# Attention scores from stacked key halves in two fp32r passes, in a two-layer decoder trunk

## The chip, the cores and the metric

The kernel runs on one core of a Trainium2 chip. Its engines run their own instruction streams side by side: TensorE (PE, matmuls; PEld are its weight loads), VectorE (DVE), ScalarE (ACT), GpSimd (POOL) and SyncE (SP), which issues most DMAs. GpSimd and ScalarE issue some too, each on a queue of its own. The metric is the device time of one execution in microseconds (us).

## The reference

Two layers over 512 tokens of width 1024. Each normalizes `x`, projects it to 3088 columns, splits them among three mixers (differential attention, a short gated convolution, gated linear attention), projects the three outputs back and adds them; then a PEER layer with 16384 single-neuron experts follows. What the change touches is the differential attention: four heads, each with two queries and two keys of 64 (index `m`), blocks of 128 queries, causal.

```python
for i in range(DEPTH):
    h = rmsnorm(x, norm_mix[i])
    proj = h @ w_in[i]
    ...
    # per block of 128 queries, 4 heads h, 2 halves m of 64:
    s = einsum('bqhmd,bkhmd->bhmqk', qi, k) * 64 ** -0.5
    p = softmax(where(mask, s, -inf), axis=-1)
    a = p[:, :, 0] - lam * p[:, :, 1]
    o_da = rmsnorm(einsum('bhqk,bkhe->bqhe', a, v), gain) * out_scale
    ...
    x = x + concatenate([o_da, o_sc, o_g]) @ w_out[i]
    x = x + peer(rmsnorm(x, norm_ffn[i]), peer_w_q[i], ...)
return rmsnorm(x, norm_final)
```

## The kernel before

Nearly all products are made from rounded and low halves: `split` (L83) rounds an F32 tile to fp32r on ACT (the high half) and subtracts it from the tile on DVE (the low half), and `mm3` (L77) contracts high x high, high x low and low x high, three fp32r matmuls for one F32 product (L79 to L81). The scores are an exception: they are one plain F32 call, which PE runs as two matmul instructions.

The mixer of a layer streams `w_in` in slabs of 256 columns. `slab` loads four pieces of a slab on SP's queue and splits them; `across` contracts a slab, 48 matmuls of 512 columns into two `psp` tiles; `down` does the same with tokens on the partitions. First come the slabs of the gated linear attention, whose own steps (`gla`, its matmuls at L610 to L680) are woven in by `fill`; then those of the queries and keys, written to `qT` and `kT` (partitions: the 64 entries of half 0 and then those of half 1; free: head, token), with a rotation of their first entries by copies on GpSimd's queue (`rope_pack`, `rope`, L459 to L471); then the values `va`; and then three slabs of the convolution, 2048, 1792 and 1536. Between these three stands the attention of blocks 0 and 1, with the scores of two heads of block 2. After them comes the output projection: `woraw` (two buffers) takes 128 rows of `w_out` at a time, split into `woh` and `wol`; blocks 2 and 3 of the attention run meanwhile, `head_out` turns the heads (`htr`) and splits them into `mh` and `ml`, and `out_proj` adds the products (`pso`) to `x`. The norm and the query projection of the PEER layer (`uraw` split into `uwa` or `uwb`, matmuls into `psq`) follow at once.

For a block and a head, `head_weights` (L479) makes the scores of both halves. The two halves lie on different partitions of `qT` and `kT`; to contract 128 partitions, `turned_queries` (L473) copies the 64 rows of a half into `qz`, whose other 64 rows are zero (filled once a layer, L369), so the keys of the other half meet zeros. A bfloat16 matmul of the identity with `causal` adds the mask (L487). DVE takes the maximum of each row, ACT the exponential.

The program is written in the order above, but each engine's order is made when the program is built: a scheduler merges the streams by what they depend on. SBUF is handed out by pools: a pool that closes gives its addresses to pools that open later, and the first writer of such an address waits for the last user of what lay there. `qT`, `kT` and `va` are in the pool `mix` (L226), which lasts for the whole mixer; the pools of the slabs close before `wout` (L404) opens.

Of the kernel before, what the change touches and what calls it, by code (L numbers as in the profile page):

```python
# [7 lines left out]
F32 = mybir.dt.float32  # L8
F32R = mybir.dt.float32r
# [10 lines left out]
P = 128  # L20
T = 512
# [46 lines left out]
class K:  # L68
# [152 lines left out]
    def mixer(self, L):  # L221
        nc, tc, ins = self.nc, self.tc, self.ins
        lam_init = 0.8 - 0.6 * math.exp(-0.3 * L)
        right = ExitStack()
        with ExitStack() as mc:
            mp = mc.enter_context(tc.tile_pool(name="mix", bufs=1, reuse_waits="tile"))  # L226
            dgain = mp.tile([P, 1], F32, name="dgain")
            cw = mp.tile([P, 2, 3], F32, name="cw")
            qT = mp.tile([P, 4, T], F32, name="qT")
            kT = mp.tile([P, 4, T], F32, name="kT")  # L230
            va = mp.tile([P, TB, T], F32, name="va")
            if L == 0:
                hh, hl = self.new_act()
                rows = lambda t: [t[:, 2 * i:2 * i + 2].rearrange("p a b -> p (a b)") for i in range(2)]
                norm = self.norm_T(ins["norm_mix"][L:L + 1, :], hh, hl, rows(va) + rows(kT), order=ORDER)
            else:
                hh, hl = self.hh, self.hl
            with ExitStack() as wc:
                wp = wc.enter_context(tc.tile_pool(name="wpool", bufs=2, reuse_waits="tile"))
                qp = wc.enter_context(tc.tile_pool(name="qkn", bufs=2, reuse_waits="tile"))  # L240
                mo = right.enter_context(tc.tile_pool(name="mixo", bufs=1, side="right", reuse_waits="tile"))
# [26 lines left out]
                def across(c0, n=256):  # L268
                    wh, wl = slab(c0, n)
                    for j in range(n // P):  # L270
                        ps = self.psC.tile([P, T], F32, tag="c", name="psp")
                        for k in range(KD):
                            self.mm3(ps, wh[:, k, j * P:j * P + P], wl[:, k, j * P:j * P + P], hh[:, k], hl[:, k],
                                     k == 0, k == KD - 1)
                        yield j, ps
# [15 lines left out]
                for i, tb in enumerate(ORDER):  # L291
                    if L:
                        ps = self.psv.pop(tb)
                    else:
                        next(norm, None)
                        ps = self.psC.tile([P, 256], F32, tag="c", name="psv")
# [18 lines left out]
                lam = mp.tile([P, 1], F32, name="lam")  # L315
# [4 lines left out]
                for tb in range(TB):  # L320
                    ps = self.psC.tile([P, 272], F32, tag="c", name="psp")
# [10 lines left out]
                side = self.gla(L, gq, gk, gv, sg, lr, mgh, mgl, gp)  # L332
# [13 lines left out]
                for i in range(4):  # L346
                    dst, h = (qT, kT)[i // 2], i % 2
# [16 lines left out]
                gc.close()  # L364
                ac = mc.enter_context(ExitStack())
                ap = ac.enter_context(tc.tile_pool(name="attn", bufs=2, side="right", reuse_waits="tile"))
                qz = [ap.tile([P, 4, 2, P], F32, name=f"qz{i}", bufs=1) for i in range(2)]
                for t in qz:
                    nc.gpsimd.memset(t, 0.0)  # L369
                heads = []  # L370

                def attend(tb, early=()):
                    heads.append(self.diff_attention(tb, qT, kT, va, qz[tb % 2], lam, ap, early))

                attend(0)
                z = qp.tile([P, 2, T + 2], F32, tag="z", name="z", bufs=1)
                nc.vector.memset(z[:, :, 0:2], 0.0)
                for j, ps in across(2048):
                    nc.scalar.copy(z[:, j, 2:], ps)
                attend(1)  # L380
                for j, ps in across(1792):
                    nc.vector.tensor_tensor(z[:, j, 2:], ps, z[:, j, 2:], op=OP.mult)
                nc.sync.dma_start(cw, ins["conv_w"][L])
                ys = []
                yt = qp.tile([P, 2, T], F32, tag="y", name="y", bufs=1)
# [6 lines left out]
                    ys.append(y)  # L392
                for j, ps in across(1536):
                    if j == 0:
                        self.turned_queries(2, qT, qz[0])
                        early = [self.head_weights(2, h, kT, qz[0], lam, ap) for h in range(2)]
                    nc.vector.tensor_tensor(ys[j], ys[j], ps, op=OP.mult)
                    self.split(mch[:, j], mcl[:, j], ys[j])

            with tc.tile_pool(name="wout", bufs=1, reuse_waits="tile") as op_:  # L400
# [31 lines left out]
                for tb in range(TB):  # L432
                    if tb > 1:
                        attend(tb, early if tb == 2 else ())
                    t = slice(tb * P, tb * P + P)
                    self.head_out(heads[tb], dgain, mh[:, 0:4, t], ml[:, 0:4, t])
# [33 lines left out]
            for m in range(2):  # L470
                nc.gpsimd.dma_start(dst[64 * m:64 * m + 16, 2 * h:2 * h + 2], rot[32 * h + 16 * m:32 * h + 16 * m + 16])  # L471

    def turned_queries(self, tb, qT, qz):  # L473
        s = slice(tb * P, tb * P + P)
        for m in range(2):
            r = slice(64 * m, 64 * m + 64)
            self.nc.scalar.copy(qz[r, :, m], qT[r, :, s])

    def head_weights(self, tb, h, kT, qz, lam, ap):  # L479
        nc = self.nc  # L480
        nk = (tb + 1) * P
        st = self.sm.tile([P, 8], F32, tag="st", name="st")
        pss = []
        for m in range(2):
            ps = self.psA.tile([P, T], F32, tag="a", name="pss")
            nc.tensor.matmul(ps[:, 0:nk], qz[:, h, m], kT[:, h, 0:nk], start=True, stop=False)  # L486
            nc.tensor.matmul(ps[:, tb * P:nk], self.identb, self.causal, start=False, stop=True)  # L487
            nc.vector.tensor_reduce(st[:, m:m + 1], ps[:, 0:nk], axis=AX.X, op=OP.max)
            pss.append(ps)
        nc.vector.tensor_scalar(st[:, 2:4], st[:, 0:2], -0.125, None, op0=OP.mult)  # L490
        e = ap.tile([P, 2, T], F32, tag="e", name="e")
        for m in range(2):
            nc.scalar.activation(e[:, m, 0:nk], pss[m][:, 0:nk], AF.Exp, bias=st[:, 2 + m:3 + m],
                                 scale=0.125, accum_out=st[:, 4 + m:5 + m])
        nc.vector.reciprocal(st[:, 6:8], st[:, 4:6])
        nc.vector.tensor_tensor(st[:, 7:8], st[:, 7:8], lam, op=OP.mult)
        nc.vector.tensor_scalar(e[:, 1, 0:nk], e[:, 1, 0:nk], st[:, 7:8], None, op0=OP.mult)
        nc.vector.scalar_tensor_tensor(e[:, 0, 0:nk], e[:, 0, 0:nk], st[:, 6:7], e[:, 1, 0:nk],
                                       op0=OP.mult, op1=OP.subtract)
        return e  # L500

    def diff_attention(self, tb, qT, kT, va, qz, lam, ap, early=()):
        nc = self.nc
        early = list(early)
        if not early:
            self.turned_queries(tb, qT, qz)
        po = self.psB.tile([P, 4, P], F32, tag="b", name="po")
        for h in range(4):
            e = early.pop(0) if early else self.head_weights(tb, h, kT, qz, lam, ap)
            tr = self.psB.tile([P, 4, P], F32, tag="b", name="atr")  # L510
            for kb in range(tb + 1):
                nc.tensor.transpose(tr[:, kb], e[:, 0, kb * P:kb * P + P], self.ident)
            aT = ap.tile([P, 4, P], F32, tag="aT", name="aT")
            nc.scalar.copy(aT[:, 0:tb + 1], tr[:, 0:tb + 1])
            for kb in range(tb + 1):
                nc.tensor.matmul(po[:, h], aT[:, kb], va[:, kb, h * P:h * P + P],
                                 start=(kb == 0), stop=(kb == tb))
        return self.head_norm(po, 4, P, ap)
# [763 lines left out]
```

## Time and profile before

| | |
|---|---|
| median of 3 runs | 2962.35 us (2961.81 to 2962.88) |
| profiled execution | 2958.37 us |
| its span, first to last instruction | 2956.6 us, clock 0.999 |
| busy: PE, DVE, ACT, POOL | 2925.6, 2394.7, 1256.3, 716.0 us |
| scores (first start in layer 0, last in layer 1) | 150.8 to 1682.2 us |

A row of a timeline has start, length (from the start of the first to the end of the last of its instructions), engine, line, operation, names written and read, shape and count; in brackets stand idle time before it and what ended that. Starts and lengths are us. A matmul's length includes the time that its result is still under way, so the pace of the engine is read from start to start. Windows give busy time of each engine in a stretch. In the groups of the page, idle time on an engine that is not the bottleneck costs nothing.

### The profile page before, as it was taken

What the parts mean: (1) busy time and instruction counts of PE and PEld (TensorE: products, weight loads), DVE (VectorE), ACT (ScalarE), POOL (GpSimd) and SP (SyncE); (2) the same over time, 40 slices, a digit from 0 to 9 for tenths busy, and PEclk for the clock granted to TensorE, in tenths of its full rate; (3) what the DMA queues carried; (4) which work ended last, traced back from release to release, by engine and by line L of the source; (5) the groups of instructions that cost most, each with busy time, mean ns of one, the idle gap of its engine ahead of it and who ended that gap; (6) DMA issues with size and microseconds to landing.
All of it is one profiled execution on the core that took longest, in us unless ns stands there. A gap on an engine that the chain in (4) does not pass through costs nothing.

```text
span 2956.6 us, 44538 instructions
## 1 busy us (share of the span) xinstructions
PE 2925.6 (99%) x16262; PEld 2606.0 (88%) x16262; DVE 2394.7 (81%) x4754; ACT 1256.3 (42%) x1860; POOL 716.0 (24%) x617
## 2 busy tenths in 40 slices
PE   8999999999999999999999999999999999999998
PEld 7878899999999999888888788999999999988887
DVE  6676999976887788877866769999768787888778
ACT  6253355665333332333453433556653333333333
POOL 1200000222444455222012000012225444452220
PEclk9999999999999999999999999999999999999999
DMA  4322257999999998999633222679999999989995
GB/s 130 92 72 77 93 172 250 321 301 362 348 338 326 330 346 310 368 333 342 251 96 90 67 82 86 205 253 330 303 351 356 333 337 332 332 316 358 346 347 203
DMA packets 335835, 760.24 MB, mean 257 GB/s; under 512 B 30688, under 2 KB 191360, under 8 KB 331520
## 3 DMA queue, kind: packets, MB, share of 16 engines
q1 hardware_dynamic: 160624, 435.19, 41.4%
q0 software_dynamic: 75776, 271.62, 26.0%
q10 hardware_dynamic: 99216, 50.60, 5.7%
q8 instruction: 127, 2.08, 0.3%
q14 instruction: 92, 0.75, 0.1%
HBM read 673.15 MB, written 81.00 MB: 255 GB/s over the span
## 4 chain that ended last, share of the span: by engine, by line
PE 84%; DVE 11%; ACT 2%; issue 2%; DMA 1%; SPq 0%; DVEq 0%; ACTq 0%
PE pv L80 11%; PE pv L81 11%; PE pv L79 11%; PE psh L79 9%; PE psh L81 9%; PE psh L80 9%; PE psp L80 2%; PE psp L81 2%; PE psp L79 2%; PE psq L80 2%; PE psq L79 2%; PE psq L81 2%; PE pss L486 1%; PE psg L1211 1%; PE pss L764 1%
## 5 line engine op out<-in xcount | busy, mean ns | idle before, releaser
L827 POOL DMA_INDIRECT row<-in_u_rows,idx x256 | 349.1, 1363 | 1337.6 <-DVE row L834 627.8
L80 PE MATMUL pv<-vl,wh 128*128 128x512 f32 x1500 | 583.9, 389 | 0.4 <-DVE vl L931 0.3
L81 PE MATMUL pv<-vh,wl 128*128 128x512 f32 x1500 | 583.4, 389 | 0.0
L79 PE MATMUL pv<-vh,wh 128*128 128x512 f32 x1500 | 583.2, 389 | 0.0
L827 POOL DMA_INDIRECT row<-in_v_rows,idx x256 | 315.7, 1233 | 597.0 <-DVE yacc L843 548.2
L745 ACT ACTIVATE ht<-psh 128x384 f32<-128x384 f32 x256 | 125.7, 491 | 742.1 <-PE psh L81 741.9
L931 DVE TENSOR_TENSOR vl<-vraw,vh 128x1024 fp32r<-128x1024 f32 x250 | 305.9, 1224 | 115.2 <-ACT vh L936 104.2
L79 PE MATMUL psh<-ahi,uwb 128*128 128x384 f32 x1024 | 346.9, 339 | 0.0
L79 PE MATMUL psh<-ahi,uwa 128*128 128x384 f32 x1024 | 346.4, 338 | 0.0
L81 PE MATMUL psh<-ahi,uwa 128*128 128x384 f32 x1024 | 344.6, 337 | 0.7 <-DVE uwa L730 0.7
L80 PE MATMUL psh<-alo,uwa 128*128 128x384 f32 x1024 | 344.3, 336 | 0.0
L80 PE MATMUL psh<-alo,uwb 128*128 128x384 f32 x1024 | 344.2, 336 | 0.0
L81 PE MATMUL psh<-ahi,uwb 128*128 128x384 f32 x1024 | 344.1, 336 | 0.0
L81 PEld LDWEIGHTS pv<-vh,wl 128*128 128x128 f32 x1500 | 281.4, 188 | 59.6 <-DVE wl L931 1.0
L80 PEld LDWEIGHTS pv<-vl,wh 128*128 128x128 f32 x1500 | 281.4, 188 | 56.6 <-DVE vl L931 2.2
L79 PEld LDWEIGHTS pv<-vh,wh 128*128 128x128 f32 x1500 | 281.6, 188 | 53.9
L843 DVE SCALAR_TENSOR_TENSOR yacc<-row,wk,yacc 128x1024 f32<-128x1024 f32 x254 | 325.2, 1280 | 1.7
L944 ACT CAST wh<-ht 128x384 fp32r<-128x384 f32 x250 | 127.9, 512 | 433.6 <-DVE ht L1096 417.0
L834 DVE SCALAR_TENSOR_TENSOR row<-row,xg 128x1024 f32<-128x1024 f32 x256 | 308.0, 1219 | 0.0
L730 DVE TENSOR_TENSOR uwa<-uraw,uwa 128x1024 fp32r<-128x1024 f32 x144 | 175.7, 1223 | 134.7 <-ACT uwa L729 134.5
L936 ACT CAST vh<-vraw 128x1024 fp32r<-128x1024 f32 x250 | 262.6, 1050 | 9.7 <-DMA vraw<-in_v_rows 9.7
L730 DVE TENSOR_TENSOR uwb<-uraw,uwb 128x1024 fp32r<-128x1024 f32 x144 | 175.8, 1222 | 105.9 <-ACT uwb L729 105.9
(361 smaller groups left out, 5708.6 us busy)
## 6 DMA issues: line engine op xcount, KB each, us to landing
uraw<-in_peer_u SPq DMA_DIRECT2D x256, 512.0 KB, 5.6
vraw<-in_v_rows SPq DMA_DIRECT2D x256, 512.0 KB, 6.5
G<-stg ACTq DMA_DIRECT2D x48, 1024.0 KB, 7.6
g<-G SPq DMA_DIRECT2D x32, 1536.0 KB, 10.0
H<-ht SPq DMA_DIRECT2D x144, 192.0 KB, 4.7
ht<-H SPq DMA_DIRECT2D x144, 192.0 KB, 6.5
wraw<-in_w_in SPq DMA_DIRECT2D x84, 256.0 KB, 3.2
uraw<-in_peer_w_q SPq DMA_DIRECT2D x32, 512.0 KB, 3.5
```

The source lines that it names most:

```text
L79: mm(ps, ah, bh, start=first, stop=False)
L80: mm(ps, ah, bl, start=False, stop=False)
L81: mm(ps, al, bh, start=False, stop=last)
L486: nc.tensor.matmul(ps[:, 0:nk], qz[:, h, m], kT[:, h, 0:nk], start=True, stop=False)
L730: self.last = pin(nc.vector.tensor_tensor(lo, src, hi.bitcast(F32), op=OP.subtract))
L745: pin(nc.scalar.activation(hs[c], ps, AF.Gelu))
L827: nc.gpsimd.indirect_dma_start(out=r, out_offset=None, in_=ins[name], in_offset=bass.IndirectOffsetOnAxis(ap=idx[:, k:k + 1], axis=0))
L834: nc.vector.scalar_tensor_tensor(r, r, 1.0, xg, op0=OP.mult, op1=OP.mult, accum_out=hd[:, k:k + 1])
L843: nc.vector.scalar_tensor_tensor(yacc, r, wk[:, k:k + 1], yacc, op0=OP.mult, op1=OP.add)
L931: self.last = pin(nc.vector.tensor_tensor(lo, src, hi.bitcast(F32), op=OP.subtract))
L936: pin(nc.scalar.copy(vh[c], vs[c]))
L944: pin(nc.scalar.copy(wh[c], hs[c]))
```

## The change

The zero-padded `qz` and its fills go. In their place, keys and queries are split, and the halves are stacked:

- `stack_keys(tb)` splits the keys of a block. For each half `m`, tile `ks[m]` has the rounded keys on the half's own 64 partitions; the low keys, subtracted into `klo`, are moved to the other 64 partitions by a DMA that GpSimd issues.
- `stack_queries(tb)` rounds the queries into `qa` on the half's own partitions, copies them by such a DMA to the other 64, and leaves the low queries in `qb`.
- The scores of a half are then two fp32r matmuls: `qa` with `ks[m]` over 128 partitions, which is rounded queries x (rounded + low keys), and `qb` with `ks[m]` over the 64 partitions of that half alone, which is low queries x rounded keys. Low x low is left out, as in `mm3`. The mask's matmul stays.

`qT` and `kT` move from `mix` to a pool `rawqk` that closes with the slabs. The attention of block 0 is written after slab 2048, that of block 1 after slab 1792.

```diff
-            qT = mp.tile([P, 4, T], F32, name="qT")
-            kT = mp.tile([P, 4, T], F32, name="kT")
             va = mp.tile([P, TB, T], F32, name="va")
+            wc = mc.enter_context(ExitStack())
+            raw_qk = wc.enter_context(tc.tile_pool(name="rawqk", bufs=1, reuse_waits="tile"))
+            qT = raw_qk.tile([P, 4, T], F32, name="qT")
+            kT = raw_qk.tile([P, 4, T], F32, name="kT")
...
-            with ExitStack() as wc:
+            with wc:
...
-                qz = [ap.tile([P, 4, 2, P], F32, name=f"qz{i}", bufs=1) for i in range(2)]
-                for t in qz:
-                    nc.gpsimd.memset(t, 0.0)
+                ks = [ap.tile([P, 4, T], F32R, name=f"ks{i}", bufs=1) for i in range(2)]
+                kl = wc.enter_context(tc.tile_pool(name="klow", bufs=2, side="right", reuse_waits="tile"))
+                half = [slice(64 * m, 64 * m + 64) for m in range(2)]
+
+                def stack_keys(tb):
+                    t = slice(tb * P, tb * P + P)
+                    lo = kl.tile([P, 4, P], F32R, tag="klo", name="klo")
+                    for m in range(2):
+                        r = half[m]
+                        self.split(ks[m][r, :, t], lo[r], kT[r, :, t])
+                        nc.gpsimd.dma_start(ks[m][half[1 - m], :, t], lo[r])
+
+                def stack_queries(tb):
+                    qa = ap.tile([P, 2, 4, P], F32R, tag="qa", name="qa")
+                    qb = ap.tile([P, 4, P], F32R, tag="qb", name="qb")
+                    for m in range(2):
+                        r = half[m]
+                        self.split(qa[r, m], qb[r], qT[r, :, tb * P:tb * P + P])
+                        nc.gpsimd.dma_start(qa[half[1 - m], m], qa[r, m])
+                    return qa, qb
+
                 heads = []
+                qs = {}
...
-                attend(0)
+                stack_keys(0)
+                qs[0] = stack_queries(0)
+                stack_keys(1)
+                qs[1] = stack_queries(1)
                 z = qp.tile([P, 2, T + 2], F32, tag="z", name="z", bufs=1)
                 nc.vector.memset(z[:, :, 0:2], 0.0)
                 for j, ps in across(2048):
                     nc.scalar.copy(z[:, j, 2:], ps)
-                attend(1)
+                attend(0)
+                for tb in (2, 3):
+                    stack_keys(tb)
+                qs[2] = stack_queries(2)
                 for j, ps in across(1792):
                     nc.vector.tensor_tensor(z[:, j, 2:], ps, z[:, j, 2:], op=OP.mult)
+                attend(1)
+                qs[3] = stack_queries(3)
...
                 for j, ps in across(1536):
                     if j == 0:
-                        self.turned_queries(2, qT, qz[0])
-                        early = [self.head_weights(2, h, kT, qz[0], lam, ap) for h in range(2)]
+                        early = [self.head_weights(2, h, ks, qs[2], lam, ap) for h in range(2)]
...
-    def head_weights(self, tb, h, kT, qz, lam, ap):
+    def head_weights(self, tb, h, ks, qs, lam, ap):
...
-            nc.tensor.matmul(ps[:, 0:nk], qz[:, h, m], kT[:, h, 0:nk], start=True, stop=False)
+            r = slice(64 * m, 64 * m + 64)
+            nc.tensor.matmul(ps[:, 0:nk], qs[0][:, m, h], ks[m][:, h, 0:nk], start=True, stop=False)
+            nc.tensor.matmul(ps[:, 0:nk], qs[1][r, h], ks[m][r, h, 0:nk], start=False, stop=False)
             nc.tensor.matmul(ps[:, tb * P:nk], self.identb, self.causal, start=False, stop=True)
```

PE, the first scores of layer 0 (`pss`; `psp` is slab 2048), before:

```order
674 L79 MATMUL psp<-ahi,wh 128x512
675 L486 MATMUL pss<-kT,qz_1503 128x128
676 L487 LDWEIGHTS identb
677 L487 MATMUL pss<-causal,identb 128x128
678 L80 MATMUL psp<-alo,wh 128x512
679 L486 MATMUL pss<-kT,qz_1503 128x128
680 L487 LDWEIGHTS identb
681 L487 MATMUL pss<-causal,identb 128x128
```

and the first scores in the change:

```order
705 L80 MATMUL psp<-alo,wh 128x512
706 L81 MATMUL psp<-ahi,wl 128x512
707 L509 MATMUL pss<-ks_1506,qa 128x128
708 L510 MATMUL pss<-ks_1506,qb 128x128
709 L511 LDWEIGHTS identb
710 L511 MATMUL pss<-causal,identb 128x128
711 L509 MATMUL pss<-ks_1507,qa 128x128
712 L510 MATMUL pss<-ks_1507,qb 128x128
713 L511 LDWEIGHTS identb
714 L511 MATMUL pss<-causal,identb 128x128
```

Before, the first scores stood between matmuls of slab 2048; now all 48 of that slab are ahead of them, and a pair has a second pass before its mask.

POOL, the end of layer 0's mixer (`kT<-rot` is the end of the keys' rotation, `row` the gathers of the PEER layer); in the change:

```order
49 L499 DMA kT<-rot 16x2x512 x4
50 L387 DMA qa<-qa 64x512
51 L379 DMA ks_1506<-klo 64x4x128
52 L379 DMA ks_1507<-klo 64x4x128
53 L387 DMA qa<-qa 64x512
54 L379 DMA ks_1506<-klo 64x4x128
55 L379 DMA ks_1507<-klo 64x4x128
56 L387 DMA qa<-qa 64x512 x2
```

Where these and eight more copies stand, two fills of `qz` stood before.

ACT, from the norm ahead of the PEER layer to its first weights (`ahi` is the rounded normalized `x`), with the semaphores of what each instruction waits for, before:

```order
184 L211 CAST ahi<-psn 128x4x128 [waits PE_49] x2
185 L729 CAST uwa<-uraw 128x1024 [waits DMAHW5_49]
186 L729 CAST uwa<-uraw 128x1024 [waits DMAHW6_49]
187 L729 CAST uwb<-uraw 128x1024 [waits DMAHW7_49,PE_49]
188 L729 CAST uwb<-uraw 128x1024 [waits DMAHW0_49,PE_49]
```

and in the change:

```order
194 L211 CAST ahi<-psn 128x4x128 [waits PE_49] x2
195 L751 CAST uwa<-uraw 128x1024 [waits DMAHW5_49,PE_49]
196 L751 CAST uwa<-uraw 128x1024 [waits DMAHW6_49,PE_49]
197 L751 CAST uwb<-uraw 128x1024 [waits DMAHW7_49]
198 L751 CAST uwb<-uraw 128x1024 [waits DMAHW0_49]
```

The order of the casts is the same; the first two wait for PE now, where the third and fourth did.

More of the change, by code (lines that the diff above doesn't have):

```diff
@@ L366, in mixer @@
                 ap = ac.enter_context(tc.tile_pool(name="attn", bufs=2, side="right", reuse_waits="tile"))
-                qz = [ap.tile([P, 4, 2, P], F32, name=f"qz{i}", bufs=1) for i in range(2)]
-                for t in qz:
-                    nc.gpsimd.memset(t, 0.0)
+                ks = [ap.tile([P, 4, T], F32R, name=f"ks{i}", bufs=1) for i in range(2)]
[16 more added lines that the diff above has]
+                    return qa, qb
                 heads = []
+                qs = {}
                 def attend(tb, early=()):
-                    heads.append(self.diff_attention(tb, qT, kT, va, qz[tb % 2], lam, ap, early))
-                attend(0)
+                    heads.append(self.diff_attention(tb, qs.pop(tb), ks, va, lam, ap, early))
+                stack_keys(0)
+                qs[0] = stack_queries(0)
+                stack_keys(1)
+                qs[1] = stack_queries(1)
                 z = qp.tile([P, 2, T + 2], F32, tag="z", name="z", bufs=1)
@@ L471, in rope @@
                 nc.gpsimd.dma_start(dst[64 * m:64 * m + 16, 2 * h:2 * h + 2], rot[32 * h + 16 * m:32 * h + 16 * m + 16])
[L473 to L477, printed above, removed]
-    def head_weights(self, tb, h, kT, qz, lam, ap):
+    def head_weights(self, tb, h, ks, qs, lam, ap):
         nc = self.nc
@@ L500, in head_weights, with diff_attention @@
         return e
-    def diff_attention(self, tb, qT, kT, va, qz, lam, ap, early=()):
+    def diff_attention(self, tb, qs, ks, va, lam, ap, early=()):
         nc = self.nc
         early = list(early)
-        if not early:
-            self.turned_queries(tb, qT, qz)
         po = self.psB.tile([P, 4, P], F32, tag="b", name="po")
         for h in range(4):
-            e = early.pop(0) if early else self.head_weights(tb, h, kT, qz, lam, ap)
+            e = early.pop(0) if early else self.head_weights(tb, h, ks, qs, lam, ap)
             tr = self.psB.tile([P, 4, P], F32, tag="b", name="atr")
```

## The prediction

> **What bounds the kernel now.** I read the page first, then the chain that ended last, then busy time by stage, then what TensorE (PE) waits for.
>
> ```profile
> PE   2925.6 (99%) x16262; PEld 2606.0 (88%) x16262; DVE 2394.7 (81%) x4754; ACT 1256.3 (42%) x1860; POOL 716.0 (24%) x617
> PE 84%; DVE 11%; ACT 2%; issue 2%; DMA 1%; SPq 0%; DVEq 0%; ACTq 0%
> 170.00:180.00 10.00, 10.00 (x55) 7.64 (x55) 7.84 (x23) 5.17 (x15) 0.00 (x0) 1.00 0.01 2
> 200.00:210.00 10.00, 9.38 (x48) 5.88 (x47) 9.24 (x21) 7.07 (x17) 0.00 (x0) 1.00 0.31 100
> PE pso L79 <- ACT woh L84: 0.9, 2, 0.6
> ```
>
> PE is busy for 99% of the span and carries 84% of the chain. The windows (PE, weight loads, DVE, ACT, POOL, granted clock, DMA share) say the same of the stage that the change touches: around the scores of layer 0 PE works 9.4 to 10.0 of every 10 us at clock 1.00, while DVE reaches 9.24 later on. The last row is PE's longest wait in layer 1's stage, for a cast of an output weight. So whatever PE gains or loses in the scores reaches the end nearly whole, and a cast that comes late costs PE directly.
>
> **The scores on PE.** 64 pairs (8 of each width, 2 layers) change. Today a pair is one F32 call, which PE runs as two matmuls, and the causal matmul in bfloat16. Columns: start, length, shape, count.
>
> ```profile
> 151.61 0.44 PE L486 MATMUL pss<-kT,qz 128*128 128x128 f32 x2
> 151.94 0.44 PE L486 MATMUL pss<-kT,qz 128*128 128x128 f32 x2
> 164.08 0.65 PE L486 MATMUL pss<-kT,qz 128*128 128x256 f32 x2
> 164.62 0.65 PE L486 MATMUL pss<-kT,qz 128*128 128x256 f32 x2
> 188.64 0.86 PE L486 MATMUL pss<-kT,qz 128*128 128x384 f32 x2
> 189.39 0.86 PE L486 MATMUL pss<-kT,qz 128*128 128x384 f32 x2
> 202.72 1.02 PE L486 MATMUL pss<-kT,qz 128*128 128x512 f32 x2
> 203.63 1.08 PE L486 MATMUL pss<-kT,qz 128*128 128x512 f32 x2
> 380.16 0.34 PE L80 MATMUL psh<-alo,uwa 128*128 128x384 f32 x1
> 380.33 0.34 PE L81 MATMUL psh<-ahi,uwa 128*128 128x384 f32 x1
> 268.57 0.39 PE L81 MATMUL pso<-woh,ml 128*128 128x512 f32 x1
> 268.80 0.28 PE L79 MATMUL psq<-ahi,uwa 128*128 128x256 f32 x1
> ```
>
> Start to start, a pair takes 0.33, 0.54 and 0.75 us at 128, 256 and 384 columns: 0.21 for each 128 columns, and 0.12 fixed (the causal matmul and its load). At 512 that line gives 0.96; the row shows 0.91, its first matmul being 0.06 shorter than the second. An fp32r pass takes 0.17 at 384 and 0.23 at 512 (the last four rows): 0.058 for each 128 columns. Two passes and the fixed part would be 0.12 + 0.115 per 128 columns: 0.235, 0.35, 0.465, 0.58.
>
> But the second pass (`qb`) contracts only 64 partitions, so PE goes from 128 rows to 64 and back in each pair. Before has such a change of rows in the gated linear attention, between L610 (128 rows) and L648 (64 rows). The tile rows give min/median/max ns; "identb" is the causal matmul's weight.
>
> ```profile
> 86.61 0.81 PE L610 MATMUL pst<-qs,ks 128*128 128x256 f32 x3
> 87.35 0.70 PE L648 MATMUL psu<-gv,kdT 64*128 64x256 f32 x2
> 87.97 0.92 PE L610 MATMUL pst<-qs,ks 128*128 128x256 f32 x3
> L610 PE MATMUL pst<-qs,ks x96: 378/379/483, 62.9 to 1584.4; 128*128 128x256 f32 x96
> L648 PE MATMUL psu<-gv,kdT x28: 376/428/480, 72.6 to 1557.9; 64*128 64x256 f32 x28
> L487 PEld LDWEIGHTS <-identb x64: 96/98/100, 150.9 to 1682.2; 128*128 128x128 bf16 x64
> ```
>
> Three L610 matmuls take 0.81 with 0.38 for the last, so 0.215 from one to the next, and three should hold PE 0.645. The 64-row matmul starts after 0.74: 0.095 of draining. Of the two L648 matmuls the first is long (480 against 376 ns: 0.10 of load that nothing hides), and L610 starts 0.62 later: 0.43 of work, 0.10 of load, 0.09 of draining again. Back at 128 rows the group is 0.92 instead of 0.81: 0.11 more of load. There and back is 0.40 us. The way back now meets the causal weight, whose load takes 98 ns where the F32 one takes about 190, so I take 0.08 off: 0.32 a pair.
>
> That makes 0.555, 0.67, 0.785 and 0.90, against 0.33, 0.54, 0.75 and 0.96: +0.225, +0.13, +0.035 and -0.06, together +0.33, times 16 = **+5 us**. Bounds: without any such cost the four differences are -0.095, -0.19, -0.285 and -0.38, so -15; with the full 0.40, and the 128-column passes at 0.11 instead of 0.058, 5 + 5 + 2 = +12. I take +5, because the nearest row has exactly this change of rows.
>
> [...]
>
> **The halves.** The F32 copies `qz` (L477, ACT) and their two zero fills (POOL) go; 16 casts on ACT and 16 subtractions on DVE come per layer, and 16 shifts of 128 KB on GpSimd's queue. The first scores wait for them; they stand after all 48 matmuls of slab 2048 now, where they stood among them.
>
> ```profile
> 146.38 0.87 PE htr L701 x8
> 148.05 1.67 ACT L84 CAST wh<-wraw 128x512 fp32r<-128x512 f32 x3
> 149.60 2.54 ACT L477 COPY qz<-qT 64x512 f32<-64x512 f32 x4
> 148.95 1.89 DVE L85 TENSOR_TENSOR wl<-wraw,wh 128x512 fp32r<-128x512 f32 x3
> 134.14 0.50 POOL L471 DMA_DIRECT2D kT<-rot  x1 [0.41 <-issue]
> rot<-qT POOLq DMA_DIRECT2D x8, 64.0 KB, 4.3
> row<-in_u_rows,idx POOLq DMA_INDIRECT x256, 7.1
> L827 POOL DMA_INDIRECT row<-in_v_rows,idx x256 | 315.7, 1233 | 597.0 <-DVE yacc L843 548.2
> ```
>
> PE starts slab 2048 at 146.38 + 0.87 = 147.25 and reaches the scores at 147.25 + 48 x 0.23 = 158.3. The first four casts follow the three weight casts, from 149.6 to about 152.1 (the copies that go took 2.54). DVE's first two subtractions follow its three (0.63 each, of the same length), from 150.85 to 152.1. The first four shifts are issued from 151.5 on at 0.50 each; the third waits for the second subtraction, so the fourth goes out at 152.6 to 153.1 and lands 4.3 later, at 157.4 at the latest. That is 0.9 before PE asks: 0, with little cover; layer 1 has the same code and is taken alike. The 16 extra DVE operations (about 10 us a layer) find room where DVE is 7.8 of 10 busy. Price if the cover goes: rival 2.
>
> **The peer weights.** Closing `qT` and `kT` with the slabs moves what lies in that memory. In before, the first two peer weights fall on memory that is free early; in the change ACT's first two such casts wait for PE, that is for the last output matmul, as the ACT order shows.
>
> ```profile
> 263.26 2.01 ACT L729 CAST uwa<-uraw 128x1024 fp32r<-128x1024 f32 x2
> 268.77 2.00 ACT L729 CAST uwb<-uraw 128x1024 fp32r<-128x1024 f32 x2 [3.49 <-PE pso L80]
> 269.85 1.23 DVE L730 TENSOR_TENSOR uwb<-uraw,uwb 128x1024 fp32r<-128x1024 f32 x1 [2.78 <-ACT uwb L729]
> 269.03 0.28 PE L81 MATMUL psq<-ahi,uwa 128*128 128x256 f32 x1
> ```
>
> Today the casts at 263.26 are done 4 us before `psq` begins at 268.80, and only the third and fourth weight wait for PE, off its path. In the change the first weight takes that place: cast at 268.77, low half ready at 269.85 + 1.23 = 271.08. PE's third `psq` matmul is the first to read it, at 269.03 today. **+2.1 us a layer, +4.2.** The second weight is ready 1.2 later, when PE still has 22 matmuls of the first to do. Bounds: 0 if the wait were already met when PE comes, 4.6 if the two matmuls ahead of it save nothing (271.08 - 268.80 = 2.3 a layer).
>
> **The output projection.** `attend(1)` moves past slab 1792, the transposes and `mh` casts of blocks 0 and 1 come later on ACT, and the last four weight casts come ahead of an `mh` cast where three did.
>
> ```profile
> 197.92 1.26 ACT L536 ACTIVATE mh<-htr,dgain 128x512 fp32r<-128x512 f32 x2
> 202.58 1.05 ACT L84 CAST woh<-woraw 128x1024 fp32r<-128x1024 f32 x1
>   DMA woraw<-in_w_out: 4.5, 4
> ```
>
> The weights pass through two buffers: a cast that starts later frees its buffer later, and ACT already waits 4.5 us for their loads in layer 0. At worst the eight transposes (0.87), the two `mh` (1.26) and a cast (1.05) all come before the chain: 3.2 a layer. At best the chain starts where it does today: 0. I take half, 1.5 a layer, **+3**.
>
> Sum: 5 + 0 + 4.2 + 3 = **+12 us**. On the profiled execution's own 2958.37 that is 2970.4; the runs shown have a median of 2962.35, 4 us above, so I predict **2974 us**.
>
> **Rivals.**
>
> 1. *The 64-row pass costs no switch.* Then PE's term is -15, the peer weights' 4.2 and the chain's 3 stay, and -8 gives 2954; the weight chain, which doesn't get shorter with PE, keeps perhaps 2 of it: 2956 (2951 to 2962). It decides if the spacing of 512-column pairs falls below about 0.7 us. Against it stand the L610 and L648 rows; for it, only that those work on F32 operands, not fp32r. This one ends on the other side. Chance 0.15.
>
> 2. *Late halves.* If the shifts behave like the gathers on the same queue (issue 1.23, landing 7.1), the fourth lands at 151.5 + 4 x 1.23 + 7.1 = 163.5, and PE, with nothing else queued but scores and what follows them, loses 163.5 - 158.3 = 5.2 a layer: 2974 + 10.4 = 2984. It decides once issue and landing pass 6.8 us. Against it: plain copies of this queue land in 4.3. [...] Chance 0.13. [...]
>
> 3. *Costs met by slack.* The chain's term is 0, since the loads of the weights set its pace as before, and a third of the switch stays hidden: 0.1 less on 64 pairs is 6.4. 5 - 6.4 + 4.2 is +2.8: 2965 (2962 to 2968). Chance 0.10.
>
> The forecast has 0.62, its own range 2966 to 2982 (scores 0 to +10, chain 0 to +6). The range is 2958 to 2988: it takes in rivals 2 and 3 and the upper part of rival 1. Below 0.2%, about 6 us, this kernel's runs cannot tell a change. Faster than 2956.4 is half of rival 1: 0.08. Within 6 us lie the rest of it, rival 3 and the lower edge of the forecast: 0.20. Slower: 0.72.
>
> **What would show it.** Right: 128-column pairs spaced near 0.55 us and 512-column pairs near 0.90; `qb` matmuls of 64 rows that begin some 0.09 late, and whose own length and that of the next show a load; DVE named as what the first `psq` group waits for, about 2 us a layer; no wait of PE ahead of the first `pss`; a longer wait for `woh`. Wrong: pairs at 0.24 to 0.58 (rival 1), PE idle ahead of the first `pss` for a DMA (rival 2), or no wait at `psq`, which would mean that the memory fell otherwise than I read it.

## The result

| | change | before, same chip |
|---|---|---|
| median | 2991.62 us (2985.91 to 2994.67, 5 runs) | 2961.81 us (2956.89 to 2962.88, 5 runs) |
| ratio | 1.010, 95% interval 1.0086 to 1.0115 | |
| profiled execution, span | 2985.91 us, 2984.1 us | 2958.37 us, 2956.6 us |

The change is slower, as forecast, but by 30 us and not by 12, and outside the range. In the profiled spans it is 27.5 us. The profiled execution of the change is the fastest of its five: its mean granted clock is 0.996, that of the others 0.993 or 0.994. One execution further down, the profiled one of the kernel with attention later, took 5928.84 us; it is slow for a reason that no run shows and is in no figure here.

The page of the change, the first part, and after it PE's waits over the whole span (in total, times, longest):

```profile
span 2984.1 us, 44664 instructions
PE 2938.7 (98%) x16262; PEld 2612.4 (88%) x16262; DVE 2410.4 (81%) x4786; ACT 1267.1 (42%) x1876; POOL 733.9 (25%) x645
...
PE pss L509 <- ACT e L517: 5.6, 2, 3.3
PE pso L79 <- ACT woh L84: 3.8, 4, 1.5
PE psq L79 <- ACT uwa L751: 1.8, 2, 0.9
PE psq L81 <- DVE uwa L752: 1.5, 2, 0.8
```

PE is busy 13 us longer and idles 14 us longer. Of the four rows of waits the last two were forecast (the late peer weight), the wait for `woh` in part; the first, for the exponentials, was not. The windows of 10 us show something else that the prediction had no term for (columns: stretch, length, busy PE, weight loads, DVE, ACT, POOL, granted clock, DMA share, GB/s):

```profile
160.00:170.00 10.00, 6.65 (x26) 4.84 (x26) 7.16 (x27) 4.31 (x17) 1.75 (x3) 0.79 0.55 106
170.00:180.00 10.00, 10.00 (x42) 7.77 (x41) 5.95 (x20) 2.63 (x9) 0.52 (x1) 0.87 0.07 14
200.00:210.00 10.00, 8.59 (x42) 5.78 (x40) 8.96 (x29) 3.82 (x11) 0.00 (x0) 1.00 0.00 0
210.00:220.00 10.00, 10.00 (x45) 6.82 (x46) 7.19 (x17) 6.03 (x14) 0.00 (x0) 0.83 0.31 104
```

The clock was 1.00 in all these stretches before; two of them, before:

```profile
160.00:170.00 10.00, 10.00 (x49) 7.44 (x49) 7.57 (x28) 5.60 (x16) 0.00 (x0) 1.00 0.10 29
210.00:220.00 10.00, 10.00 (x44) 6.53 (x43) 9.56 (x24) 6.06 (x12) 0.00 (x0) 1.00 0.47 162
```

Now it falls behind pauses of PE, to 0.79 and 0.87 behind the first and to 0.83 from 210 us on, and a "busy" 10.00 then holds fewer matmuls (42 from 170 to 180 us, 55 before). In steps of 2 us behind the first pause:

```profile
164.00:166.00 2.00, 1.35 (x7) 0.97 (x7) 1.33 (x6) 2.00 (x10) 0.00 (x0) 0.97 0.07 20
166.00:168.00 2.00, 2.00 (x9) 1.46 (x8) 1.93 (x10) 0.77 (x2) 0.14 (x1) 0.50 0.00 0
168.00:170.00 2.00, 2.00 (x8) 1.67 (x7) 1.13 (x4) 1.16 (x6) 0.40 (x1) 0.50 0.35 66
170.00:172.00 2.00, 2.00 (x7) 1.71 (x6) 1.44 (x6) 1.50 (x6) 0.52 (x1) 0.50 0.00 0
172.00:174.00 2.00, 2.00 (x9) 1.45 (x8) 0.85 (x4) 0.08 (x1) 0.00 (x0) 0.83 0.35 66
```

About 6.8 us at half clock: 3.4 us of work lost, as much as the pause itself took. The half-clock stretches of layer 0 last 6.83 us from 165.86 us on and 3.41 us from 210.24 us on; the pauses ahead of them are 3.35 us, and 0.65 and 0.62 us close together.

I added up windows of 2 us over both stages (140 to 300 and 1620 to 1790 us): PE's time without work, and its busy time times what the clock fell short of 1.00.

| | layer 0: idle, lost to clock | layer 1 | both, against before |
|---|---|---|---|
| before | 1.6, 0.0 | 2.2, 0.0 | |
| change | 9.0, 5.1 | 8.4, 5.1 | idle +13.6, clock +10.2 |

With +3.8 for the score pairs themselves (below) that is 27.6 us, against the 27.5 us of the spans.

The pairs came out as forecast. Their starts in the change:

```profile
158.31 0.30 PE L509 MATMUL pss<-ks,qa 128*128 128x128 f32 x1
158.55 0.32 PE L510 MATMUL pss<-ks,qb 64*128 64x128 f32 x1
158.80 0.23 PE L511 MATMUL pss<-causal,identb 128*128 128x128 bf16 x1
158.84 0.31 PE L509 MATMUL pss<-ks,qa 128*128 128x128 f32 x1
...
205.70 0.42 PE L509 MATMUL pss<-ks,qa 128*128 128x384 f32 x1
206.05 0.44 PE L510 MATMUL pss<-ks,qb 64*128 64x384 f32 x1
206.42 0.23 PE L511 MATMUL pss<-causal,identb 128*128 128x128 bf16 x1
206.46 0.42 PE L509 MATMUL pss<-ks,qa 128*128 128x384 f32 x1
```

0.53 us at 128 columns and 0.76 at 384. Over all 64 pairs, each from its first matmul to what follows the mask, the medians are 0.53, 0.60, 0.78 and 0.87, against 0.33, 0.52, 0.76 and 0.94 before: 44.5 against 40.7 us for all.

Where the first pause comes from is read on ACT, the rows of halves and weights in order, and then on PE:

```profile
149.37 1.27 ACT L84 CAST ks<-kT 64x512 fp32r<-64x512 f32 x2
...
155.14 2.54 ACT L84 CAST ks<-kT 64x512 fp32r<-64x512 f32 x4
157.70 1.14 ACT L84 CAST wh<-wraw 128x512 fp32r<-128x512 f32 x2
...
159.22 0.62 ACT L84 CAST wh<-wraw 128x512 fp32r<-128x512 f32 x1
163.62 0.62 ACT L84 CAST wh<-wraw 128x512 fp32r<-128x512 f32 x1 [3.78 <-DMA wraw<-in_w_in]
164.15 0.36 ACT L517 ACTIVATE e<-pss,st 128x128 f32<-128x128 f32 x1
```
```profile
164.65 0.33 PE L509 MATMUL pss<-ks,qa 128*128 128x128 f32 x1 [3.35 <-ACT e L517]
```

The same weight cast before, and the first exponential behind it:

```profile
152.58 0.62 ACT L84 CAST wh<-wraw 128x512 fp32r<-128x512 f32 x1 [0.44 <-DMA wraw<-in_w_in]
153.10 0.36 ACT L493 ACTIVATE e<-pss,st 128x128 f32<-128x128 f32 x1
```

Twelve casts of halves stand ahead of the weight cast at 157.70; before, it ran at 152.58. With DVE's subtraction behind it (158.45 to 159.14) it frees the buffer of the next load, which SP issues at 159.17 instead of 153.95 and which lands 4.45 us later (the third piece of slab 1536; before, such loads took 2.7 to 3.5). In layer 1 that load takes 3.4 us, and PE's wait is 2.2 us. ACT waits for that load, and the exponentials of block 0, which need nothing of it, stand behind in ACT's order, though the maxima that they wait for are done by 161.8 and 162.8. PE has four score buffers, all full, and its next instruction is the fifth pair.

### The profile page after: what moved, and what is told of

The parts are those of the page before. It is cut to its first block, busy times and chain, and to the rows that moved or that the text cites. A ratio compares the mean times of both kernels' runs of the same rounds, so it can differ in the third digit from the quotient of the medians.

```text
span 2984.1 us, 44664 instructions
## 1 busy us (share of the span) xinstructions
PE 2938.7 (98%) x16262; PEld 2612.4 (88%) x16262; DVE 2410.4 (81%) x4786; ACT 1267.1 (42%) x1876; POOL 733.9 (25%) x645
## 4 chain that ended last, share of the span: by engine, by line
PE 86%; DVE 9%; ACT 2%; DMA 2%; issue 1%; SPq 0%; ACTq 0%; DVEq 0%
PE pv L80 11%; PE pv L81 11%; PE pv L79 11%; PE psh L79 10%; PE psh L81 10%; PE psh L80 10%; PE psp L81 2%; PE psp L80 2%; PE psp L79 2%; PE psq L79 2%; PE psq L80 2%; PE psq L81 2%; PE psg L1233 1%; PE psg L1234 1%; PE pss L786 1%
```

## The experiments

The theories at first: **A**, ACT's order makes a pause and the clock doubles its price; **B**, the changes between 64 and 128 rows; **C**, the copies between partitions crowd the loads.

**The halves of blocks 1 to 3 later.** Their casts are held behind slab 1792's weights and what was traced before.

```diff
+                def cast(hi, lo, src, late):
+                    c = nc.scalar.copy(hi, src)
+                    if late:
+                        tc.keep_in_program_order(c)
+                    nc.vector.tensor_tensor(lo, src, hi.bitcast(F32), op=OP.subtract)
...
                 for j, ps in across(1792):
+                    if j == 0:
+                        stack_keys(1)
+                        qs[1] = stack_queries(1)
+                    else:
+                        stack_keys(2)
...
```

> The change, with only the halves of block 0 split ahead of slab 1792's weights; the casts of blocks 1 to 3 are held behind those weight casts and the exponentials traced before them on ACT. Theory A (ACT's order): in the change the fourth piece of slab 1792 is cast at 157.7 us behind 12 casts of halves, so the next load is issued at 159.17 instead of 153.95, the cast that waits for it stands ahead of block 0's exponentials, PE idles 3.35 us for them and the clock is then halved for some 7 us (3.4 us lost). Held back, the stall and the halved clock go in both layers: about 13 us less than the change, some 15 above before. Theory B (the 64-row pass is what costs): no difference, within 2 us of the change. Theory C (the shift copies crowd the loads): the stall stays for the most part, 0 to 4 us less.

2987.42 us (before in its group 2959.94; ratio 1.0085, 1.0068 to 1.0102): 4 us less than the change, not 13. The first pause is gone, and with it the drop behind it; but another pause comes 40 us later, where block 2's maxima wait on DVE behind the held subtractions, and it costs the clock more:

```profile
160.00:170.00 10.00, 9.54 (x49) 6.62 (x49) 6.91 (x31) 5.61 (x24) 0.00 (x0) 1.00 0.28 51
200.00:210.00 10.00, 8.24 (x29) 5.34 (x29) 7.65 (x21) 5.75 (x15) 0.00 (x0) 0.57 0.30 98
...
200.46 0.45 PE L517 MATMUL pss<-ks,qa 128*128 128x384 f32 x1 [1.09 <-ACT e L525]
```

So A names the first pause rightly, but the loss moves. A gain of 4 us is also the end of C's range, but C had the first pause stay.

**The second pass over 128 rows.**

```diff
-            nc.tensor.matmul(ps[:, 0:nk], qs[1][r, h], ks[m][r, h, 0:nk], start=False, stop=False)
+            nc.tensor.matmul(ps[:, 0:nk], qs[1][:, h], ks[m][:, h, 0:nk], start=False, stop=False)
```

> The change, with the second pass over all 128 partitions: the low queries of both halves against the stacked keys of one, which adds low queries of the other half x low keys, a term of the size of the low x low that is left out anyway. No 64-row matmul is left in the scores. Theory B: pairs fall from about 0.53, 0.60, 0.76 and 0.87 us to 0.24, 0.35, 0.47 and 0.58, 17 us in all, and the time falls by 15 to 20. Theory A: the pairs fall the same, but PE then comes earlier to the stall for block 0's exponentials, which is not its own making, so 8 to 14 us of it reach the end.

The order of PE, ACT, DVE and POOL is that of the change. 2973.43 us (before 2959.94; 1.0044, 1.0027 to 1.0061): 18 us less than the change, inside B's range, above A's. The pairs take 0.32, 0.32, 0.49 and 0.59, 27.6 us in all, 16.9 less than in the change. Two of 384 columns, 0.47 apart:

```profile
199.59 0.42 PE L508 MATMUL pss<-ks,qa 128*128 128x384 f32 x1
199.84 0.33 PE L509 MATMUL pss<-ks,qb 128*128 128x384 f32 x1
200.02 0.23 PE L510 MATMUL pss<-causal,identb 128*128 128x128 bf16 x1
200.06 0.42 PE L508 MATMUL pss<-ks,qa 128*128 128x384 f32 x1
```

So the change of rows costs 0.26 us a pair, and what it costs reaches the end. But even with pairs that are 13 us cheaper than F32 ones the kernel stays 13.5 above before: PE idles 11.0 and 10.7 us a layer, and 7.3 us go to the clock.

**The first peer weight early.** The two `uwa` buffers become tags of their own, and the first is laid out ahead of `uraw`, over the values' memory.

```diff
+            def new_uwa(shape, dt, name):
+                i = turns[0] % 2
+                turns[0] += 1
+                return self.up.tile(shape, dt, tag=f"uwa{i}", name=name, bufs=1)
+
+            early_w = [new_uwa([P, 2, KD, P], F32R, "uwa")]
```

> The change, with the first peer weight placed over the values' memory instead of over the turned heads', so that its split need not wait for the last output matmul. The term of the late peer weights says: PE's waits of 0.9 and 0.8 us at the first psq matmuls and the 1.3 us between the first psq and the first psh go, 2.4 us a layer, 4 to 5 in all, if the third weight's load, which now waits instead, is in time. If that wait has cover elsewhere: no difference.

2995.32 us (before 2959.94; 1.0113, 1.0096 to 1.0129): no gain, 4 above the change. The first `psq` now follows the last `pso` by 0.2 us, as before the change, but the load of the third weight lies over the turned heads' memory, and PE waits for that weight. Waits of PE in this stage of layer 0:

```profile
PE psq L79 <- ACT uwa L760: 1.7, 1, 1.7
PE psq L81 <- DVE uwa L761: 0.8, 1, 0.8
```

From the first `psq` to the first `psh` it takes 109.5 us, 2.0 more than in the change. The term itself is in the change's trace; this run moved the wait to another weight and did not take it away.

**No copies between partitions.**

```diff
-                        nc.gpsimd.dma_start(ks[m][half[1 - m], :, t], lo[r])
-                        nc.gpsimd.dma_start(qa[half[1 - m], m], qa[r, m])
+                qas = [ap.tile([P, 2, 4, P], F32R, name=f"qa{i}", bufs=1) for i in range(2)]
+                for t in ks + qas:
+                    nc.gpsimd.memset(t.bitcast(F32), 0.0)
```

> The change without the 32 copies between partitions: the other partitions of the keys and of the rounded queries are filled with zeros once a layer, so rounded queries x low keys is left out of the scores; casts, subtractions and matmuls are as in the change. Theory C: the load that lands 4.4 us after its issue in the change lands in 2.9 as before, and the stall goes with its halved clock: 10 to 14 us less than the change. Theory A: the load's issue stays late at about 159, so the stall shrinks from 3.35 to about 2 us and the clock still drops: 0 to 5 us less.

2983.1 us (before 2959.94; 1.0067, 1.005 to 1.0084): 8 us less than the change, between the two expectations. PE's wait ahead of the fifth pair is gone, yet not by C's way: the cast that waited for the load comes even later, at 165.78 where the change has 163.62, but without the copies the build put the exponentials ahead of it (161.27 to 163.10). Other pauses keep 4.9 and 3.1 us of lost clock. This run doesn't separate A from C.

**Pauses put into the kernel before.** The cast of the first peer weight is repeated, so that PE has a pause at the first `psq`, whose length is set by the count. Behind it the first cast of `uwb` comes later too.

```diff
+            again = [1 + (6, 8)[L]]          # second kernel: (7, 10)
...
-                pin(nc.scalar.copy(hi, src))
+                for _ in range(again.pop() if again else 1):
+                    pin(nc.scalar.copy(hi, src))
```

> The kernel before, with the cast of the first peer weight repeated on ACT ahead of its use (6 more times in layer 0, 8 in layer 1), so that PE, with nothing else to do, waits some 2.2 us at the first psq of layer 0 and 4.4 in layer 1. If a stall costs its own length alone, the stages from the last pso to the first psh grow by 2.2 and 4.4 us and the granted clock stays at 1.00. If the clock drops after a stall, as it did in the change, some 3.4 or 6.8 us at half clock follow, and each stage grows by 1.7 or 3.4 us more.

> The same with 7 and 10 repeats: waits of 3.3 and 6.6 us. Without an effect on the clock the stages grow by 3.3 and 6.6; with it, 3.4 to 6.8 us at half clock follow both, and they grow by 1.7 to 3.4 us more each.

One run each: 2968.56 and 2972.36 us (before 2960.9), spans 10.2 and 14.0 us above before's profiled one. PE's waits, one row of each kernel, and layer 1 of the first in windows of 2 us:

```profile
PE psq L79 <- ACT uwa L732: 6.5, 4, 4.0
...
1740.00:1742.00 2.00, 0.38 (x2) 0.00 (x0) 0.00 (x0) 1.94 (x3) 0.00 (x0) 1.00 0.00 0
1742.00:1744.00 2.00, 0.00 (x0) 0.00 (x0) 0.00 (x0) 1.94 (x3) 0.00 (x0) 0.64 0.00 0
1744.00:1746.00 2.00, 1.43 (x5) 1.14 (x6) 1.60 (x2) 2.00 (x3) 0.00 (x0) 0.50 0.00 0
1746.00:1748.00 2.00, 2.00 (x11) 2.00 (x11) 2.00 (x3) 0.26 (x1) 0.00 (x0) 0.50 0.70 197
1748.00:1750.00 2.00, 2.00 (x14) 2.00 (x13) 0.75 (x3) 1.23 (x3) 0.00 (x0) 0.65 0.79 234
```
```profile
PE psq L79 <- ACT uwa L732: 9.6, 3, 6.2
```

| pause at psq (grown by) | 2.1 | 3.2 | 4.2 | 6.4 us |
|---|---|---|---|---|
| busy time lost to the clock behind it | 1.6 | 1.5 | 2.4 | 3.0 us |

Waits and lost clock together, 6.3 + 4.0 and 9.6 + 4.5 us, are the 10.2 and 14.0 of the spans. These four pauses of PE, 2.1 to 6.4 us, cost themselves and 1.5 to 3 us behind them. The stretches at half clock are 3.41 and 6.83 us long in the first kernel, 3.41 and 10.24 in the second; in layer 1 they begin while PE still waits, as the window from 1742 shows (clock 0.64, PE idle), and what of them falls into the pause costs nothing.

**The kernel before, attention later.** Blocks 0 and 1 stand where the change has them; scores stay F32.

```diff
-                attend(0)
                 ...
                 for j, ps in across(2048):
                     nc.scalar.copy(z[:, j, 2:], ps)
-                attend(1)
+                attend(0)
                 for j, ps in across(1792):
                     nc.vector.tensor_tensor(z[:, j, 2:], ps, z[:, j, 2:], op=OP.mult)
+                attend(1)
```

> The kernel before, with only the place of the attention of blocks 0 and 1 as in the change: after slabs 2048 and 1792. F32 scores, qz and the memory stay. If the later place alone takes PE's cover away in the output projection, PE idles more between the last psp and the last pso, the clock drops there, and the time rises by 6 to 12 us. If the halves' casts and copies are what makes the stalls, it stays within 3 us of before.

2958.21 us (ten runs; before 2960.9; ratio 0.9991, 0.9982 to 1.0001): the place alone costs nothing.

**Halves for blocks 2 and 3 only.** Blocks 0 and 1 keep F32 scores and their old place; blocks 2 and 3 use the 128-row passes.

```diff
+            if tb < 2:
+                nc.tensor.matmul(ps[:, 0:nk], qs[:, h, m], ks[:, h, 0:nk], start=True, stop=False)
+            else:
+                nc.tensor.matmul(ps[:, 0:nk], qs[0][:, m, h], ks[m][:, h, 0:nk], start=True, stop=False)
+                nc.tensor.matmul(ps[:, 0:nk], qs[1][:, h], ks[m][:, h, 0:nk], start=False, stop=False)
```

> F32 scores on qz for blocks 0 and 1, in the place they had before; stacked halves, with the second pass over 128 rows, for blocks 2 and 3 alone, so that 12 copies a layer are left and none is waited for early. Pairs of 384 and 512 columns fall by 0.28 and 0.36 us, 10 us in all. If PE's work still sets the end: 2955 to 2962, with the late peer weights' 4 to 5 us in it. If the output weights' casts set the pace once PE is faster, that gain is lost to waits for woh and wol and to the halved clock: 2962 to 2970.

2970.47 us (before 2960.9; 1.0029, 1.0018 to 1.0039), half a us above the second expectation. The pairs together take 31.0 us instead of 40.7, so 9.7 were gained and 19 lost: PE idles 7.2 and 5.2 us more and loses 3.3 and 3.4 us to the clock. Its waits name the output weights first:

```profile
PE pso L79 <- ACT woh L84: 5.1, 5, 1.6
PE atr L544 <- DVE ml L569: 3.0, 2, 1.5
```

**The halves' work beside F32 scores.** To the kernel with attention later the casts and subtractions of the halves are added, into tiles that nothing reads; then the copies too.

```diff
+                    for m in range(2):
+                        r = half[m]
+                        self.split(hi[r], lo[r], src[r, :, t])
+                        to = kl.tile([P, 4, P], F32R, tag="to", name=name + "to", bufs=4)     # second kernel
+                        nc.gpsimd.dma_start(to[half[1 - m]], (lo if name == "k" else hi)[r])  # second kernel
```

> The kernel of the run before_late (F32 scores, blocks 0 and 1 a slab later) with the 16 casts and 16 subtractions of the halves a layer added at the change's places; their results go to tiles that nothing reads, and there are no copies between partitions. If the split work on ACT and DVE is what makes the stalls, PE idles 2 to 5 us more a layer, the clock drops, and the time is 8 to 20 us above before_late's. If the copies or the wait for them make the stalls: within 3 us of it.

> The same with the 16 copies a layer on GpSimd's queue too, into tiles that nothing reads. If their traffic delays the loads of weights, the time is 3 us or more above that of the splits alone, with later landings of wraw; if not, the two are equal within 2 us.

2962.27 us (before 2960.97; 1.0004, 0.9995 to 1.0014) and 2964.96 us (1.0011, 1.0002 to 1.0021): 1 and 4 us above before, some 4 and 6 above the kernel with attention later. The first lies between its two expectations, and so does the second, 2.7 us above the first; as the engines' orders differ between the two, that difference isn't the copies' alone. In these builds the exponentials stand ahead of the cast that waits. PE does pause, 1.4 us a layer, but here the clock stays up:

```profile
160.00:170.00 10.00, 8.27 (x46) 6.22 (x45) 9.44 (x35) 9.81 (x31) 4.08 (x8) 1.00 0.67 126
...
PE pss L513 <- ACT e L520: 2.9, 2, 1.4
```

So the work of the halves, even with its copies, doesn't cost 30 us by itself. In the change it stands between the scores and what they wait for. That this place makes the pauses is read from the traces; no run took all of them away and got the time back.

**Both edits.** Later halves and the 128-row pass.

> The change with both edits: halves of blocks 1 to 3 split behind slab 1792's weights, and the second pass over 128 rows. If the two edits add up: 18 and 4 us less than the change, about 2969. If a faster PE only waits longer for the exponentials and the output weights: 2971 to 2980. If the first stall's halved clock is gone for good: 2960 to 2966.

2976.3 us (before 2960.97; 1.0053, 1.0036 to 1.0069): no better than the 128-row pass alone (2973.43), in the middle expectation. PE idles 11.6 and 11.0 us a layer.

**The exponentials ahead of the waiting cast.** In the change the last two pieces of slab 1536 are held behind the fourth exponential of block 0. Up to that exchange ACT's order is the same; behind it the build also moved the last two query casts and some steps of DVE and PE.

```diff
+                        piece = nc.scalar.copy(wh[:, kh:kh + 2], raw)
+                        if behind is not None and kh >= 4:
+                            tc.add_manual_dep(piece.ins, behind, mybir.DependencyInfo(
+                                mybir.DependencyClass.NoSync, mybir.DependencyReason.DATA), reason="behind")
```

> The change with one exchange in ACT's order: the cast of the third piece of slab 1536, which waits 3.8 us for its load in the change, stands behind the exponentials of block 0's first two heads and not ahead of them. If that place is the cause of PE's 3.35 us wait and the halved clock after it: the wait falls to about 1 us or less, the clock stays at 1.00 in that stage, and the time falls by 8 to 14 us. If the wait is set by when the halves and scores are ready, or the lost time comes back in the output projection: 0 to 4 us.

2989.32 us (before 2960.29; 1.0101, 1.0082 to 1.0119): some 2 us less than the change, in the second expectation. PE's pause falls from 3.35 to 1.5 us, because the exponentials now wait for the maxima, which stand on DVE behind subtractions of keys; and that pause is enough:

```profile
161.28 0.37 ACT L523 ACTIVATE e<-pss,st 128x128 f32<-128x128 f32 x1 [1.96 <-DVE st L520]
...
160.00:170.00 10.00, 8.52 (x31) 6.23 (x30) 7.95 (x31) 5.90 (x22) 1.69 (x4) 0.66 0.46 102
210.00:220.00 10.00, 10.00 (x36) 6.13 (x35) 6.43 (x12) 3.86 (x8) 0.00 (x0) 0.66 0.34 107
```

8.2 and 5.0 us are lost to the clock, against 5.1 and 5.1 in the change. Half of the pause was the cast's; in this run its removal saved next to nothing, as the clock took more.

**That exchange with the 128-row pass.**

> Both the 128-row second pass and that exchange. If the two add up: 18 and 8 to 14 us less than the change, 2959 to 2966, level with before. If the output projection's weights set the pace by then: 2966 to 2974.

2972.75 us (before 2960.29; 1.0049, 1.0031 to 1.0067): the same as the 128-row pass alone, in the second expectation. No version that was run with stacked halves in use is faster than before.

## Why the prediction was right or wrong

- **Direction and the scores' term: right.** "There and back is 0.40 us", 0.32 a pair, and +5 in all; measured +3.8. Rival 1 (no cost of the switch) is out: taken away, the switch was worth 16.9 us in the pairs and 18 in the time. At 384 columns the 64-row pass begins 0.35 us behind the pass ahead of it, where one of 128 rows begins 0.25 behind. The weight load of the 64-row pass starts 0.35 us behind the matmul ahead of it (206.05 against 205.70); between the 128-row passes of slab 2048 the next load starts within 0.01 us of the matmul ahead of it (157.64 against 157.63). What the prediction calls draining and a load that nothing hides are its names for such gaps, 0.09 and 0.10 us at L648; how much of the 0.26 us is the one and how much the other, these runs don't separate.
- **The peer weights: right.** +2.1 us a layer was forecast; from the last `pso` to the first `psh` it takes 2.3 us more in layer 0 and 3.0 in layer 1. In layer 0 the first `psq` comes 1.1 later behind the last `pso`, and the first `psh` another 1.2 (107.6 instead of 106.3 us behind the first `psq`). PE waits for ACT's cast (0.9) as well as for DVE's low half (0.8), which alone was named. The early casts of before are done 3.5 us ahead of `psq` (263.26 + 2.01 against 268.80), not 4; nothing hangs on it.
- **The halves: the step that failed.** Their readiness was right: the first pair started at 157.86 without a wait (forecast 158.3). But "0, with little cover" asked only whether the halves reach PE in time. It did not ask what stands behind the twelve casts and the subtractions on ACT and DVE, where each waits its turn: a weight cast 5.1 us later, its load 5.2 later, and then the exponentials and maxima of scores that were done. That is the pause of 3.35 us in layer 0 and 2.2 in layer 1, where the term says 0. The prediction reasons just so about `woraw` ("a cast that starts later frees its buffer later"), but not about `wraw`. Rival 2, at 2984 us, came nearer, but not by its way: no instruction of PE waited for a copy (DVE did, 0.78 us in layer 0, for one that frees `klo`), and it put no price on the clock.
- **The clock: a term that was missing.** Lost to half clock are 10.2 us, over a third of the whole. The clock stood at 1.00 in the windows of before, and the prediction took it as given; its price hangs on PE's pauses, which the forecast added at their own length.
- **The output projection: undersized.** +3 was forecast; from the last `psp` to the last `pso` each layer takes about 4 us more (layer 0: 10.7 + 65.9 instead of 9.3 + 63.0), 1.7 of it by the drop at 210 us. A delayed chain of weight casts was part of it (PE waits 3.8 us for `woh` instead of 0.9), as argued.

Open is behind what length of pause the clock stays up. Behind 1.4 us in the kernels with the halves' work it stayed at 1.00; behind 1.5 us in the exchange, and behind two waits of 0.65 and 0.62 us close together near 209 us in the change, it halved. So it did behind 1.09 us in the run with the later halves.

The traces narrow it. In each trace that has several, the half-clock stretches start whole multiples of 3.41 us apart and last one to four times 3.41 us (in the change from 165.86, 210.24, 1647.25 and 1691.62 us, for 6.83, 3.41, 6.83 and 3.41 us); where this grid lies differs from trace to trace. I cut the traces into steps on their grids (without the first 30 and the last 12 us) and added up PE's idle time in each step at full clock. Every step with 1.67 us or more was followed by half clock, none with less than 0.64 us was, and those between went both ways. In the change 2.20 and 2.04 us were followed by half clock, 1.46 and 1.32 were not, and two steps of 1.27 were. So above 1.67 and below 0.64 us the idle time that falls into one step tells in these traces whether the clock drops; that a pause of the same length costs more or less with its place on the grid is my estimate from this, as no run moved a pause along it. What decides between 0.64 and 1.63 us stays open.

## What to carry to other kernels

PE is busy for 99% of the span of before, and here pauses of 2.1 to 6.4 us cost their length and then 1.5 to 3.4 us more, so on such an engine sum pauses with the drop of the clock behind them, and look for them wherever its partners' work grows. When work is added to an engine that takes its work in order, as ACT did here, list what stands behind it and who waits for that, not only whether the added work's own result is in time. A pass over 64 rows between matmuls over 128 costs about 0.26 us here; filling the other rows with operands that do no harm avoided that (0.47 instead of 0.76 us a pair at 384 columns). No version with halves kept that gain: PE waited elsewhere instead.

## What the runs showed of the hardware

That TensorE's clock is halved behind pauses as short as 1.09 us (the run with the later halves, for 10.24 us) and 1.5 us (the exchange, for 6.83 us) was not expected; in the kernel before a pause of 2.1 us cost 1.6 more and one of 6.4 cost 3.0 more. Nor was it expected that a second pass with all 128 rows filled is faster than one with half of them, 0.47 against 0.76 us a pair at 384 columns.
